# Rounding a kernel's weight parts in the transfer itself, and one product over both parts of the moving operand

## The chip, the core and the metric

The kernel runs on one core of a Trainium2 chip. The metric is the device time of one launch, in microseconds (us), as the median of several runs. One further execution was recorded by the hardware profiler; every duration below is from that execution. PE is the matrix engine (PEld its weight loads), DVE the vector engine, ACT the scalar engine, POOL is GpSimd, and SP issues transfers.

## What is computed

Two layers of a hybrid backbone run over 256 context tokens followed by 256 latent tokens, with width 2048, batch 1 and float32 data. Cut to what matters here:

```
def hybrid_layer(ctx_h, x, ...):
    u_l = rmsnorm(x, norm_w) * (1.0 + scale_l) + shift_l
    u_c = rmsnorm(ctx_h, norm_w) * (1.0 + scale_c) + shift_c
    lx_c, lg_c, q_c, k_c, v_c, ag_c, xbc_c, z_c, dt_c = split_cols(u_c @ w_in)
    lx_l, lg_l, q_l, k_l, v_l, ag_l, xbc_l, z_l, dt_l = split_cols(u_l @ w_in)
    ...   # a gated linear recurrence, windowed attention, a state-space mixer
    mix_l = concatenate([lru_l * silu(lg_l), att_l * silu(ag_l), ssd_l])
    x_new = x + gate_l * (mix_l @ w_out)
    if update_ctx: ctx_h = ctx_h + gate_c * (mix_c @ w_out)      # in the first layer only
```

Most of the work is `u @ w_in` (2048 by 7168, and 16 further columns for dt) and `mix @ w_out` (3072 by 2048) in each layer. The second layer returns no context tokens, so there lg, q, ag, z, the C part of xbc, and all of `w_out` are wanted for the 256 latent tokens alone.

## The kernel before

**Products in three pieces.** Tokens lie along the free dimension: 512 columns in the first layer, 512 or 256 in the second. A weight block is 128 by 128. PE's fast form of float32 rounds its operands, so both operands are cut in two: `hi`, the rounded value, and `lo`, the rest. `mm3` (L247) then makes three products into one accumulator: hi by u's high part, hi by u's low part, and lo by u's high part. Each product loads its own weights. A tile of 512 columns takes three products of 512, and one of 256 columns three of 256.

**The weight stream.** `blocks` (L233) brings weights in halves of four blocks (128 partitions by 512 numbers, 256 KB). For each half SP issues a transfer into `raw` (five buffers), ACT copies raw to `hi`, which rounds it (four buffers), and DVE subtracts `lo` = raw - hi (four buffers). A raw buffer is free once its subtraction is done; hi and lo buffers are free once PE has read them. Each layer has 224 halves of `w_in` and 96 of `w_out`, 640 in all.

**What sets the order.** PE's instructions stand in the order in which the program is written; the mixers are generators that the main loop resumes at due times (`WAIT`, `pump`) counted on a clock of PE work. On the other engines a scheduler that simulates the program at build time orders the instructions. Each engine works its queue strictly in that order: an instruction that waits holds all behind it.

**Stages of a layer.** The head takes the first column tiles of `w_in` (B, C, x) while the modulation is still being loaded; the body takes the rest (lx with lg, z, k and v, q with ag); then `w_out` runs in three parts of 16 column tiles with 8 blocks each. At the end of a `w_out` tile DVE adds the accumulator, times the gate, to the stream `X` (L1082). The mixers put work on all engines: POOL multiplies in the recurrence (L732, L744, L754), in the rotation of q (L776) and scales the attention weights `prob` (L873). Consumers of a column tile (`ssd_z`, `lru_g`, `att_q`, `att_g`) read the accumulator directly.

Of the kernel before, what the change touches and what calls it, by code (L numbers as in the profile page):

```python
# [9 lines left out]
F32R = mybir.dt.float32r  # L10
# [103 lines left out]
for _tag, _bufs, _roles in [  # L114
        ("raw", 5, ("raw",)),
# [16 lines left out]
HB = 4  # L132
# [8 lines left out]
class Kernel:  # L141
# [91 lines left out]
    def blocks(self, src, n_tiles):  # L233
        nc = self.nc
        for i in range(n_tiles):
            whole = src[i].rearrange("p (b c) -> p b c", b=8)
            for h in range(2):
                part = self.t([P, 4, P], "raw")
                nc.sync.dma_start(out=part, in_=whole[:, 4 * h:4 * h + 4])
                hi = self.t([P, 4, P], "hi", HB, F32R)  # L240
                lo = self.t([P, 4, P], "lo", HB, F32R)
                nc.scalar.activation(out=hi, in_=part, func=AF.Copy)  # L242
                nc.vector.tensor_tensor(out=lo, in0=part, in1=hi.bitcast(F32), op=ALU.subtract)  # L243
                for b in range(4):
                    yield hi[:, b], lo[:, b]

# [187 lines left out]
    def u_tile(self, shape=(P, 512)):  # L434
        return self.t(list(shape), "u", 32, F32R)

    def split(self, src, w):
        nc = self.nc
        hi, lo = self.u_tile(), self.u_tile()
        nc.scalar.activation(out=hi[:, :w], in_=src, func=AF.Copy)  # L440
        nc.vector.tensor_tensor(out=lo[:, :w], in0=src, in1=hi[:, :w].bitcast(F32), op=ALU.subtract)
        return hi, lo


    def make_u(self, k, xs, rb, mod):
# [6 lines left out]
        hi, lo = self.u_tile(), self.u_tile()  # L452
# [7 lines left out]
        return hi, lo  # L460


    def conv(self, dst, px, w, b, segs):
# [74 lines left out]
    def ssd_dt(self, l, us, wds):  # L538
        nc = self.nc
        acc = self.ada_acc()  # L540
        for k in range(KT):
            lhsT = wds[k // 8][:, 32 * (k % 8):32 * (k % 8) + P]
            self.mm(acc, lhsT, us[k][0], k == 0, False)
            self.mm(acc, lhsT, us[k][1], False, k == KT - 1)
            self.pump()
# [104 lines left out]
    def ssd_z(self, l, i, pz, t0):  # L650
        nc = self.nc
        th = self.t([P, 512], "cth")[:, t0:]
# [94 lines left out]
    def lru_g(self, l, m, pg, t0):  # L747
        nc = self.nc
        th = self.t([P, 512], "lgt", 1)[:, t0:]
# [61 lines left out]
    def att_q(self, l, h, pq, t0):  # L811
# [4 lines left out]
        sq = self.t([P, 512], "sq", 2)  # L816
        nc.scalar.activation(out=sq[:, t0:], in_=pq, func=AF.Square)
# [83 lines left out]
    def att_g(self, l, h, pg, t0):  # L901
        nc = self.nc
        th = self.t([P, 512], "agt", 1)[:, t0:]
# [10 lines left out]
    def mix_tiles(self, l, part):  # L914
# [17 lines left out]
        for k in range(8):  # L932
            load(k + 4)
            hi, lo = self.split(self.Y[:, k, w0:] if part == 2 else staged[k], n)
            yield hi[:, :n], lo[:, :n]
# [19 lines left out]
    def layer(self, l, xs):  # L955
# [7 lines left out]
        wst = self.blocks(self.a["w_in"][l], NW)  # L963
# [35 lines left out]
        for ct, ks in head_plan(l):  # L999
            fill = ct in FILL[l]  # L1000
            acc = self.mx() if fill else accs[ct][:, cols(ct)]
            for k in ks:
# [22 lines left out]
                self.mm3(acc, next(wst), us[k][0][:, cols(ct)], us[k][1][:, cols(ct)], k == (ks[0] if fill else 0),  # L1025
# [19 lines left out]
        for ct in body(l):  # L1045
# [5 lines left out]
            acc = self.acc()[:, s:]  # L1051
            for k in range(KT):
                self.mm3(acc, next(wst), us[k][0][:, s:], us[k][1][:, s:], k == 0, k == KT - 1)
# [12 lines left out]
        for pi, part in enumerate(OUT_PARTS):  # L1066
# [3 lines left out]
            for m in range(KT):  # L1070
                acc = self.acc()[:, w0:]
                for k in range(8):
                    mix = self.ahead(l, part, min(8, k + 2))[k]
                    self.mm3(acc, next(wo), mix[0], mix[1], k == 0, k == 7)
# [4 lines left out]
                for c, s in ((1, slice(0, C)), (0, slice(C, T))):  # L1079
                    if s.start < w0:  # L1080
# [201 lines left out]
```

## Time and profile before

| | |
|---|---|
| median of 3 runs | 1828.84 us (1825.97 to 1830.53) |
| profiled execution, its own time | 1825.69 us |
| span in that execution | 1823.7 us |
| mean granted share of PE's clock | 0.993 |
| HBM read, written | 310.38 MB, 10.63 MB |
| GpSimd transfers | none |

The span is what the trace covers; the profiled execution lasted 2.0 us more than its span. In the views, a line such as L175 is where the instruction was written; L175 is the helper that every product goes through, so products are told apart by the tiles they write and read: `acc<-u,hi` is a product of the weight stream's high part, `mx<-...` mostly the mixers' work. A matrix instruction's end is modelled, and consecutive ones overlap, so the rate of a stream is read from a run's length divided by its count, not from an instruction's duration. The time of the first 100 us or so is that of the loads; from there on PE has work all the time.

### The profile page before, as it was taken

The numbers are of one execution on the slowest core, as the hardware profiler recorded it, in microseconds if no ns is written. First come the engines' busy times: TensorE is split into PE (matmuls) and PEld (weight loads), VectorE is DVE, ScalarE is ACT, GpSimd is POOL, SyncE is SP. The second block draws the span as 40 slices with busy tenths as digits, with TensorE's granted clock in tenths as the row PEclk, the third lists the DMA queues.
The fourth block names the chain that finished last, engine by engine and source line by source line (L and its number), as shares of the span: only waits on it lengthen the run. The fifth ranks groups of instructions, "written<-read, shape, count | busy, mean of one in ns | idle before, by whom it ended". The sixth has DMA issues, their size and how long they took to land.

```text
span 1823.7 us, 30174 instructions
## 1 busy us (share of the span) xinstructions
PE 1762.9 (97%) x10522; PEld 1449.8 (79%) x10522; DVE 1406.0 (77%) x3117; ACT 972.9 (53%) x1798; POOL 215.5 (12%) x179
## 2 busy tenths in 40 slices
PE   7999999999999999999999999999989999999999
PEld 4677876667778778887888887888767788999999
DVE  4447769898898888889999536877788785788665
ACT  4324578688523354555232335544788863678443
POOL 0000111111110021212000020001122120121000
PEclk9999999999999999999999999999999999999999
DMA  9982333334675645557777433464343564554655
GB/s 359 389 299 66 123 104 104 122 122 144 230 222 179 189 153 184 173 174 239 229 225 225 144 122 107 140 197 148 99 134 113 173 220 137 182 180 153 218 185 179
DMA packets 186343, 322.99 MB, mean 177 GB/s; under 512 B 19120, under 2 KB 44624, under 8 KB 185552
## 3 DMA queue, kind: packets, MB, share of 16 engines
q1 hardware_dynamic: 186192, 321.09, 54.0%
q8 instruction: 82, 1.34, 0.3%
q14 instruction: 69, 0.57, 0.1%
HBM read 310.38 MB, written 10.63 MB: 176 GB/s over the span
## 4 chain that ended last, share of the span: by engine, by line
PE 71%; DVE 9%; issue 8%; ACT 6%; DMA 5%; POOL 1%; SPq 0%; ACTq 0%; DVEq 0%; POOLq 0%
PE acc L175 56%; PE mx L175 12%; PE ada L175 2%; DVE lo L243 2%; DMA bc<-acsD 2%; PE mx L171 1%; DVE araw L385 1%; ACT hi L242 1%; DVE ada L385 1%; DVE lh L735 1%; DMA araw<-in_adaw_dram 1%; DMA ar<-in_ada_dram 1%; DVE ee L1170 1%; ACT ww L1172 1%; ACT lt L717 1%
## 5 line engine op out<-in xcount | busy, mean ns | idle before, releaser
L175 PE MATMUL acc<-u,hi 128*128 128x512 f32 (+1 forms) x4800 | 1278.0, 355 | 3.8 <-ACT u L457 3.0
L175 PEld LDWEIGHTS acc<-u,hi 128*128 128x128 f32 x4800 | 837.5, 190 | 149.4 <-issue 33.2
L175 PE MATMUL acc<-u,lo 128*128 128x512 f32 (+1 forms) x2400 | 843.0, 351 | 7.9 <-DVE lo L243 7.8
L242 ACT ACTIVATE hi<-raw 128x512 fp32r<-128x512 f32 x640 | 397.5, 628 | 536.4 <-PE acc L175 401.3
L243 DVE TENSOR_TENSOR lo<-raw,hi 128x512 fp32r<-128x512 f32 x640 | 456.8, 717 | 185.9 <-ACT hi L242 175.3
L175 PEld LDWEIGHTS acc<-u,lo 128*128 128x128 f32 x2400 | 455.4, 190 | 73.1 <-DVE lo L243 12.9
L385 DVE SCALAR_TENSOR_TENSOR araw<-araw,adac 128x512 f32<-128x512 f32 x256 | 184.3, 720 | 6.2 <-DMA araw<-in_adaw_dram 3.9
L385 DVE SCALAR_TENSOR_TENSOR ada<-araw,adac 128x512 f32<-128x512 f32 x192 | 140.1, 730 | 13.2 <-DMA araw<-in_adaw_dram 6.7
L175 PE MATMUL mx<-u,hi 128*128 128x512 f32 (+1 forms) x320 | 98.8, 392 | 0.0
L1082 DVE SCALAR_TENSOR_TENSOR X<-acc,mod,X 128x256 f32<-128x256 f32 x144 | 65.0, 478 | 40.2 <-PE acc L175 40.2
L732 POOL TENSOR_TENSOR lt<-lt,ltl 128x512 f32<-128x512 f32 x32 | 45.9, 1457 | 327.2 <-ACT ltl L729 304.9
L873 POOL TENSOR_SCALAR prob<-prob,qrs 128x512 f32<-128x512 f32 (+1 forms) x48 | 58.2, 1228 | 214.0 <-ACT hi L242 123.9
L432 POOL TENSOR_TENSOR ssq<-ssq,sq 128x512 f32<-128x512 f32 (+1 forms) x26 | 34.0, 1310 | 308.1 <-ACT sq L428 308.1
L175 PEld LDWEIGHTS mx<-u,hi 128*128 128x128 f32 x320 | 55.9, 188 | 14.0 <-issue 4.6
L175 PE MATMUL mx<-u,lo 128*128 128x512 f32 (+1 forms) x160 | 60.7, 379 | 0.0
L516 POOL TENSOR_SCALAR X<-xs,prm 128x512 f32<-128x512 f32 (+1 forms) x16 | 16.3, 1024 | 362.0 <-DVE xs L494 357.5
L175 PE MATMUL mx<-xc,gw 64*64 64x512 f32 x128 | 41.7, 622 | 8.8 <-ACT lt L717 5.3
L428 ACT ACTIVATE sq<-X 128x256 f32<-128x256 f32 (+1 forms) x44 | 18.8, 452 | 54.5 <-DVE X L659 52.8
L1170 DVE SCALAR_TENSOR_TENSOR ee<-bc,nacs,ee 128x128 f32<-128x128 f32 x96 | 34.8, 418 | 14.8 <-DMA bc<-acsD 9.1
L776 POOL TENSOR_TENSOR qw<-qw,cst 128x256 f32<-128x256 f32 x20 | 23.1, 1156 | 195.6 <-DVE rt L775 168.9
L717 ACT ACTIVATE lt<-mx,gbh 128x512 f32<-128x512 f32 x64 | 42.2, 674 | 4.1 <-PE mx L175 4.0
L1169 ACT ACTIVATE ee<-bc,nacs 128x128 f32<-128x128 f32 x96 | 30.6, 391 | 17.7 <-DMA bc<-acsD 17.7
(240 smaller groups left out, 1946.1 us busy)
## 6 DMA issues: line engine op xcount, KB each, us to landing
raw<-in_w_in_dram SPq DMA_DIRECT2D x448, 256.0 KB, 2.8
araw<-in_adaw_dram SPq DMA_DIRECT2D x256, 256.0 KB, 3.1
raw<-in_w_out_dram SPq DMA_DIRECT2D x192, 256.0 KB, 3.0
ar<-in_ada_dram SPq DMA_DIRECT2D x84, 256.0 KB, 5.4
bc<-acsD SPq DMA_DIRECT2D x48, 256.0 KB, 3.9
ar<-in_ada_dram SPq DMA_DIRECT2D x22, 512.0 KB, 7.0
adac<-condD SPq DMA_DIRECT2D x28, 256.0 KB, 4.4
gw<-in_gates_dram SPq DMA_DIRECT2D x16, 256.0 KB, 2.9
```

The lines of the kernel that those rows point to most:

```text
L175: self.nc.tensor.matmul(out=out, lhsT=lhsT, rhs=rhs, start=start, stop=stop, **kw)
L242: nc.scalar.activation(out=hi, in_=part, func=AF.Copy)
L243: nc.vector.tensor_tensor(out=lo, in0=part, in1=hi.bitcast(F32), op=ALU.subtract)
L385: i = nc.vector.scalar_tensor_tensor(out=o, in0=raw, scalar=1.0, in1=row[c].rearrange("p t x -> p (t x)"), op0=ALU.mult, op1=ALU.mult, acc ...
L432: nc.gpsimd.tensor_tensor(out=self.ssq[0], in0=self.ssq[0], in1=sq, op=ALU.add)
L717: nc.scalar.activation(out=t, in_=pg[g], func=AF.Tanh, scale=0.5, bias=self.gb[:, 16 * g + 8 * d + m:16 * g + 8 * d + m + 1])
L732: nc.gpsimd.tensor_tensor(out=ti, in0=ti, in1=tl[:, d], op=ALU.mult)
L776: nc.gpsimd.tensor_tensor(out=dst, in0=src, in1=self.con("cos"), op=ALU.mult)
L873: nc.gpsimd.tensor_scalar(out=pr[j], in0=pr[j], scalar1=rs[:, j:j + 1], scalar2=1.0, op0=ALU.mult, op1=ALU.mult)
L1082: nc.vector.scalar_tensor_tensor(out=x[:, s], in0=acc[:, s.start - w0:s.stop - w0], scalar=mod[:, 2 * KT + m, c:c + 1], in1=x[:, s], op0=A ...
L1169: nc.scalar.activation(out=e[:, j], in_=bcs[0][:, j], func=AF.Identity, bias=k.nacs[:, f:f + 1])
L1170: nc.vector.scalar_tensor_tensor(out=e[:, j], in0=bcs[1][:, j], scalar=k.nacs[:, r:r + 1], in1=e[:, j], op0=ALU.add, op1=ALU.min)
```

## The change

There are two edits.

**Rounding by the transfer.** `blocks` gets a parameter `own`. For the first `own` pairs of halves ACT rounds as before; for all others GpSimd issues a second transfer of the same half, from the float32 weights in HBM straight into the float32r tile `hi`, which converts on the way. `own` is 20 for the first layer's `w_in` (40 halves, the 160 blocks of its head) and 0 elsewhere: 600 halves of 640 are fetched twice. DVE still subtracts `lo` from raw and hi. The buffers change: raw has three in place of five, hi six in place of four, lo four as before.

**One product over both parts of u.** The two parts of u now lie in one tile [128, 2, 512]. For the second layer's 256-column tiles in the body (lg, z, q, ag: 32 tiles of 16 blocks) and for all of its `w_out` (48 tiles of 8 blocks), `mm_wide` makes one product of hi with both parts, 512 columns into two halves of the accumulator, and one of lo with u's high part into the first half. The two halves are added later: by a new DVE reduction (`whole`) ahead of the consumer in the body, and by a second DVE update of X per `w_out` tile. The C tiles in the second layer's head still go through `mm3`.

```diff
-        ("raw", 5, ("raw",)),
+        ("raw", 3, ("raw",)),
...
-    def blocks(self, src, n_tiles):
+    def blocks(self, src, n_tiles, own=0):
...
                 nc.sync.dma_start(out=part, in_=whole[:, 4 * h:4 * h + 4])
-                hi = self.t([P, 4, P], "hi", HB, F32R)
-                lo = self.t([P, 4, P], "lo", HB, F32R)
-                nc.scalar.activation(out=hi, in_=part, func=AF.Copy)
+                hi = self.t([P, 4, P], "hi", 6, F32R)
+                lo = self.t([P, 4, P], "lo", 4, F32R)
+                if i < own:
+                    nc.scalar.activation(out=hi, in_=part, func=AF.Copy)
+                else:
+                    nc.gpsimd.dma_start(out=hi, in_=whole[:, 4 * h:4 * h + 4])
                 nc.vector.tensor_tensor(out=lo, in0=part, in1=hi.bitcast(F32), op=ALU.subtract)
...
+    def mm_wide(self, acc, block, u, cols, start, stop):
+        hi, lo = block
+        n = cols.stop - cols.start
+        both = lambda: self.mm(acc.rearrange("p (i t) -> p i t", i=2), hi, u[:, :, cols], start, stop)
+        if not stop:
+            both()
+        self.mm(acc[:, 0:n], lo, u[:, 0, cols], False, False)
+        if stop:
+            both()
...
+    def whole(self, acc, t0, dst):
+        if t0 == 0:
+            return acc
+        self.nc.vector.tensor_reduce(out=dst[:, 0:t0], in_=acc.rearrange("p (i t) -> p t i", i=2), axis=AX.X, op=ALU.add)
+        return dst[:, 0:t0]
...
+        pz, th = self.whole(pz, t0, th), th[:, t0:]
...
+        wst = self.blocks(self.a["w_in"][l], NW, 0 if l else 20)
...
+                if s:
+                    self.mm_wide(acc, next(wst), us[k], slice(s, T), k == 0, k == KT - 1)
+                else:
+                    self.mm3(acc, next(wst), us[k][:, 0], us[k][:, 1], k == 0, k == KT - 1)
...
+                late = slice(C, T)
+                for c, s, o in ((0, late, 0), (0, late, n)) if l else ((1, slice(0, C), 0), (0, late, C)):
+                    nc.vector.scalar_tensor_tensor(out=x[:, s], in0=acc[:, o:o + C], scalar=mod[:, 2 * KT + m, c:c + 1],
+                                                   in1=x[:, s], op0=ALU.mult, op1=ALU.add)
```

PE, in the last `w_out` tile of the second layer, before: two blocks, three products each (u's two parts are tiles of their own).

```order
L175 MATMUL acc_19442<-u_18704,hi_19445 128x256
L175 MATMUL acc_19442<-u_18705,hi_19445 128x256
L175 MATMUL acc_19442<-u_18704,lo_19446 128x256
L175 MATMUL acc_19442<-u_18710,hi_19445 128x256
L175 MATMUL acc_19442<-u_18711,hi_19445 128x256
L175 MATMUL acc_19442<-u_18710,lo_19446 128x256
```

PE at the same place after: three blocks of the same tile.

```order
L174 MATMUL acc_18553<-u_17948,hi_18556 128x512
L174 MATMUL acc_18553<-u_17948,lo_18557 128x256
L174 MATMUL acc_18553<-u_17953,hi_18556 128x512
L174 MATMUL acc_18553<-u_17953,lo_18557 128x256
L174 MATMUL acc_18553<-u_17987,hi_18556 128x512
L174 MATMUL acc_18553<-u_17987,lo_18557 128x256
```

A block has two products where it had three, over the same 768 columns.

DVE, in the second layer's `w_out`, before. The tiles' accumulators follow each other as 18623, 18667, 18715, 18763; a lo belongs to the tile whose accumulator's number is next below its own, so lo_18737 is the second half of tile 18715.

```order
L1082 SCALAR_TENSOR_TENSOR X_17512<-acc_18623,mod_33_146,X_17512 128x256
L243 TENSOR_TENSOR lo_18737<-raw_18734,hi_18736 128x512
L243 TENSOR_TENSOR lo_18767<-raw_18764,hi_18766 128x512
L1082 SCALAR_TENSOR_TENSOR X_17512<-acc_18667,mod_33_146,X_17512 128x256
L243 TENSOR_TENSOR lo_18785<-raw_18782,hi_18784 128x512
L243 TENSOR_TENSOR lo_18815<-raw_18812,hi_18814 128x512
```

DVE in the same stage after; the accumulators follow each other as 17851, 17882, 17919, 17958.

```order
L1113 SCALAR_TENSOR_TENSOR X_16968<-acc_17851,mod_33_146,X_16968 128x256
L246 TENSOR_TENSOR lo_17923<-raw_17920,hi_17922 128x512
L1113 SCALAR_TENSOR_TENSOR X_16968<-acc_17882,mod_33_146,X_16968 128x256 x2
L246 TENSOR_TENSOR lo_17937<-raw_17934,hi_17936 128x512
L246 TENSOR_TENSOR lo_17962<-raw_17959,hi_17961 128x512
L1113 SCALAR_TENSOR_TENSOR X_16968<-acc_17919,mod_33_146,X_16968 128x256 x2
```

Before, the update of tile m is followed by the second half of tile m+2; after, both updates of tile m (17882) are followed by the second half of tile m+1 (17919). The two updates stand next to each other in 31 of the 48 tiles, and around a lo in the others.

POOL, among the second layer's q tiles, before: the rotation of one head and the scaling of another's weights, in turn.

```order
L776 TENSOR_TENSOR qw_16139<-qw_16139,cst_76 128x256
L873 TENSOR_SCALAR prob_16263<-prob_16263,qrs_16262 128x512
L873 TENSOR_SCALAR prob_16265<-prob_16265,qrs_16262 128x512
L776 TENSOR_TENSOR qw_16376<-qw_16376,cst_76 128x256
L873 TENSOR_SCALAR prob_16492<-prob_16492,qrs_16491 128x512
```

POOL at such a place after; each transfer waits until PE has read the half six before it.

```order
L245 DMA hi_16464<-in_w_in_dram 128x512
L245 DMA hi_16524<-in_w_in_dram 128x512
L899 TENSOR_SCALAR prob_16286<-prob_16286,qrs_16285 128x512
L899 TENSOR_SCALAR prob_16288<-prob_16288,qrs_16285 128x512
L245 DMA hi_16555<-in_w_in_dram 128x512
L245 DMA hi_16569<-in_w_in_dram 128x512
L801 TENSOR_TENSOR qw_16388<-qw_16388,cst_76 128x256
```

The mixers' POOL work now stands between transfers for which the weight stream waits; POOL has 600 such transfers beside 174 instructions of the mixers.

## Rows read from the trace of the kernel before

**Rows 1.** Page: busy us of the engines; then GB/s in 40 slices.
```profile
PE 1762.9 (97%) x10522; PEld 1449.8 (79%) x10522; DVE 1406.0 (77%) x3117; ACT 972.9 (53%) x1798; POOL 215.5 (12%) x179
...
GB/s 359 389 299 66 123 104 104 122 122 144 230 222 179 189 153 184 173 174 239 229 225 225 144 122 107 140 197 148 99 134 113 173 220 137 182 180 153 218 185 179
```

**Rows 2.** Chain that ended last: start us, length us, engine, line, count; two runs.
```profile
...
898.55 213.56 PE acc L175 x942
...
1698.32 122.06 PE acc L175 x1017
```

**Rows 3.** Groups by form, whole span: count | busy us, mean ns.
```profile
...
L175 PE MATMUL acc<-u,hi 128*128 128x512 f32 x2976 | 943.4, 398 | 3.8 <-ACT u L457 3.0 <-DVE u L458 0.8
...
L175 PE MATMUL acc<-u,hi 128*128 128x256 f32 x1824 | 335.0, 285 | 0.0
```

**Rows 4.** Waits of PE, 100 to 1824 us: total us, times, longest us.
```profile
...
PE mx L175 <- ACT lt L717: 11.9, 8, 4.2
PE acc L175 <- DVE lo L243: 7.8, 10, 1.6
PE mx L175 <- DVE ee L1176: 4.2, 2, 3.1
...
PE mx L171 <- POOL prob L873: 3.4, 4, 2.2
...
PE mx L175 <- ACT sq L817: 0.3, 1, 0.3
```

**Rows 5.** The same view of 1440 to 1490 us alone.
```profile
...
PE acc L175 <- DVE lo L243: 4.4, 4, 1.6
```

**Rows 6.** Waits of ACT, then of DVE, 100 to 1824 us, same columns.
```profile
...
ACT hi L242 <- PE acc L175: 394.0, 277, 6.3
...
DVE lo L243 <- ACT hi L242: 149.2, 138, 3.6
```

**Rows 7.** Busy us by stretch: PE, PEld, DVE, ACT, POOL; clock, DMA share, GB/s.
```profile
...
1220.00:1440.00 220.00, 206.91 (x1189) 160.33 (x1187) 172.44 (x315) 156.38 (x281) 32.35 (x28) 0.98 0.40 129
1440.00:1490.00 50.00, 45.46 (x346) 39.43 (x345) 41.24 (x66) 40.34 (x66) 14.10 (x12) 1.00 0.62 201
1490.00:1690.00 200.00, 199.04 (x1449) 187.95 (x1449) 152.60 (x350) 128.88 (x251) 33.65 (x29) 1.00 0.54 174
1698.00:1821.00 123.00, 122.36 (x1020) 122.15 (x1018) 79.47 (x133) 53.87 (x90) 0.00 (x0) 1.00 0.60 188
```

**Rows 8.** Groups by form of 1698 to 1821 us, DVE and ACT.
```profile
...
L243 DVE TENSOR_TENSOR lo<-raw,hi 128x512 fp32r<-128x512 f32 x81 | 56.1, 692 | 29.7 <-ACT hi L242 27.4
L242 ACT ACTIVATE hi<-raw 128x512 fp32r<-128x512 f32 x81 | 51.1, 631 | 61.6 <-PE acc L175 61.6
L1082 DVE SCALAR_TENSOR_TENSOR X<-acc,mod,X 128x256 f32<-128x256 f32 x43 | 20.8, 483 | 11.9 <-PE acc L175 11.9
```

**Rows 9.** DVE in order of time: start us, length us, [idle before, releaser].
```profile
...
1751.28 0.48 DVE L1082 SCALAR_TENSOR_TENSOR X<-acc,mod,X 128x256 f32<-128x256 f32 x1 [0.20 <-PE acc L175]
1751.82 0.69 DVE L243 TENSOR_TENSOR lo<-raw,hi 128x512 fp32r<-128x512 f32 x1
```

**Rows 10.** Transfers: mean rate, us from issue to landing; 1698:1821, then 20:85.
```profile
...
DMA packets 13975, 23.12 MB, mean 188 GB/s; under 512 B 1539, under 2 KB 3971, under 8 KB 13964
...
raw<-in_w_out_dram SPq DMA_DIRECT2D x77, 256.0 KB, 3.1
...
DMA packets 11970, 24.87 MB, mean 383 GB/s; under 512 B 1339, under 2 KB 1627, under 8 KB 11961
...
raw<-in_w_in_dram SPq DMA_DIRECT2D x19, 256.0 KB, 5.7
```

**Rows 11.** POOL's dearest, a DVE reduction, SP's issues of raw (min/median/max ns).
```profile
L732 POOL TENSOR_TENSOR lt<-lt,ltl 128x512 f32<-128x512 f32 x32 | 45.9, 1457 | 327.2 <-ACT ltl L729 304.9 <-DVE araw L385 22.3
...
L851 DVE TENSOR_REDUCE qmx<-mx 128x1 f32<-128x512 f32 x32 | 20.9, 680 | 0.1
...
L239 SPq DMA_DIRECT2D raw<-in_w_out_dram x77: 327/328/489, 1697.9 to 1808.7; - x77
```

More of the change, by code (lines that the diff above doesn't have):

```diff
@@ L459, in make_u @@
                                            op0=ALU.add, op1=ALU.subtract)
[L460 removed]
+        return u
     def conv(self, dst, px, w, b, segs):
@@ L748, in lru_g @@
         nc = self.nc
-        th = self.t([P, 512], "lgt", 1)[:, t0:]
+        th = self.t([P, 512], "lgt", 1)
+        pg, th = self.whole(pg, t0, th), th[:, t0:]
         nc.scalar.activation(out=th, in_=pg, func=AF.Tanh, scale=0.5)
@@ L816, in att_q @@
         sq = self.t([P, 512], "sq", 2)
+        pq = self.whole(pq, t0, qw)
         nc.scalar.activation(out=sq[:, t0:], in_=pq, func=AF.Square)
@@ L902, in att_g @@
         nc = self.nc
-        th = self.t([P, 512], "agt", 1)[:, t0:]
+        th = self.t([P, 512], "agt", 1)
+        pg, th = self.whole(pg, t0, th), th[:, t0:]
         nc.scalar.activation(out=th, in_=pg, func=AF.Tanh, scale=0.5)
@@ L933, in mix_tiles @@
             load(k + 4)
-            hi, lo = self.split(self.Y[:, k, w0:] if part == 2 else staged[k], n)
-            yield hi[:, :n], lo[:, :n]
+            yield self.split(self.Y[:, k, w0:] if part == 2 else staged[k], n)
     def ahead(self, l, part, n):
@@ L1024, in layer @@
                         self.prms.append(self.params(1))
-                self.mm3(acc, next(wst), us[k][0][:, cols(ct)], us[k][1][:, cols(ct)], k == (ks[0] if fill else 0),
+                self.mm3(acc, next(wst), us[k][:, 0, cols(ct)], us[k][:, 1, cols(ct)], k == (ks[0] if fill else 0),
                          k == (ks[-1] if fill else KT - 1))
@@ L1050, in layer @@
                 self.att_begin(l)
-            acc = self.acc()[:, s:]
+            acc = self.acc()
             for k in range(KT):
-                self.mm3(acc, next(wst), us[k][0][:, s:], us[k][1][:, s:], k == 0, k == KT - 1)
+                if s:
+                    self.mm_wide(acc, next(wst), us[k], slice(s, T), k == 0, k == KT - 1)
+                else:
+                    self.mm3(acc, next(wst), us[k][:, 0], us[k][:, 1], k == 0, k == KT - 1)
                 if ct == ("ag", 7) and OUT_PARTS[0] in self.parts_done:
@@ L1070, in layer @@
             for m in range(KT):
-                acc = self.acc()[:, w0:]
+                acc = self.acc()
                 for k in range(8):
                     mix = self.ahead(l, part, min(8, k + 2))[k]
-                    self.mm3(acc, next(wo), mix[0], mix[1], k == 0, k == 7)
+                    if l:
+                        self.mm_wide(acc, next(wo), mix, slice(0, n), k == 0, k == 7)
+                    else:
+                        self.mm3(acc, next(wo), mix[:, 0], mix[:, 1], k == 0, k == 7)
                     self.pump()
@@ L1078, in layer @@
                 x = xs[m // 8][:, m % 8]
-                for c, s in ((1, slice(0, C)), (0, slice(C, T))):
-                    if s.start < w0:
-                        continue
-                    nc.vector.scalar_tensor_tensor(out=x[:, s], in0=acc[:, s.start - w0:s.stop - w0],
-                                                   scalar=mod[:, 2 * KT + m, c:c + 1], in1=x[:, s], op0=ALU.mult,
-                                                   op1=ALU.add)
+                late = slice(C, T)
+                for c, s, o in ((0, late, 0), (0, late, n)) if l else ((1, slice(0, C), 0), (0, late, C)):
+                    nc.vector.scalar_tensor_tensor(out=x[:, s], in0=acc[:, o:o + C], scalar=mod[:, 2 * KT + m, c:c + 1],
+                                                   in1=x[:, s], op0=ALU.mult, op1=ALU.add)
                 if pi == 2:
```

19 lines of the change are left out of this document (9 added, 10 removed).

## The prediction

> **What bounds the kernel now.** I read the busy shares first, then the chain, then who waits for whom, then single stages. PE is busy 97% of the span, DVE 77%, ACT 53%, POOL 12% [rows 1]. A busy PE can still be a slow one, so its two long undisturbed runs in the chain are the measure: 942 products of 512 columns in 213.56 us, or 0.227 us each, and 1017 of 256 columns in 122.06 us, or 0.120 us each [rows 2]. After the first 100 us PE waits little: the 15 lines of its waits, of which the first and the last stand there, sum to 43.1 us [rows 4], of which 15.2 end on ACT (11.9 of them on the gates' `lt`), 7.8 on DVE's `lo` (4.4 in the z tiles of the second layer alone [rows 5]), 16.7 on other work of DVE and 3.4 on POOL's `prob`. So the program is PE's stream plus some 43 us, and an edit gains by shortening that stream or by those waits, and by nothing else.
>
> What rounding on ACT costs is mostly not its 631 ns [rows 8]: an ACT rounding stands in a strict queue until PE gives back a hi buffer, 394.0 us in 277 waits, and DVE's `lo` then waits for ACT another 149.2 us [rows 6]. All work of the mixers behind them on ACT and DVE waits along.
>
> **One product over both parts.** A 256-column block takes 3 x 0.120 = 0.360 us now and 0.227 + 0.120 = 0.347 after, so 0.0133 us less; for 32 x 16 + 48 x 8 = 896 blocks that is 11.9 us. A product costs 13 ns beyond its columns at 2.4 GHz in both runs (0.2267 against 0.2133, 0.1200 against 0.1067), and one product in three goes. The Trainium skill's TensorE: Matmul & The Clock Gate (Back-to-back issue gap) has N/2.4 + 2.5 ns instead; by that one product less would save only 2.5 ns a block, an estimate of 2.2 us in all and a total 9.7 us later. This trace doesn't agree with the page (13 ns), and I take the trace.
>
> The 11.9 us fall in three places: 5.1 in lg, q and ag (384 blocks), 1.7 in z (128), 5.1 in `w_out` (384). In lg, q and ag they are PE's to keep, since lx or attention stand between them and leave the supply time. In the other two a half of weights is used up in 4 x 0.347 = 1.39 us, and supply has to be looked at.
>
> **Supply in z and `w_out` of the second layer.** Three limits, each per half:
> The raw buffers. A raw buffer is taken from issue to landing, 3.1 us, and through the subtraction, 0.69 us and some 0.05 between [rows 8, 10]: 3.84 us, by five buffers 0.77 us, by three 1.28 us. That is still under 1.39, but the transfers now move twice the weights: 188 GB/s there now and some 189 more (262 KB in 1.39 us), against 383 GB/s in the start, where landing took 5.7 us [rows 10]. With 5.7 us the three buffers give one half per 2.15 us. I take 3.7 us, nearer the low end, since in the start some fifteen buffers of other loads were in flight and here it is three raws and a hi or two: 1.48 us per half.
> DVE's order. It does both updates of X before the next `lo`. From the start of a tile's last product: its duration 0.398 [rows 3], two updates of 0.48 with 0.06 behind each, and 0.69 for `lo` [rows 9], 2.17 us. PE can fill 0.227 + 1.387 + 0.227 = 1.84 us of it, until the second half's `lo` is wanted. So 0.33 us are short in each of the 31 tiles where both updates come first, 10 us. Before, that `lo` was made a whole tile earlier.
> POOL's issue. The trace of before has no GpSimd transfer. The low end for one is SP's issue, 0.33 us, the high end POOL's dearest instruction, 1.457 us [rows 11]. I take 1.0; only the high end is over 1.39.
> Together: `w_out` takes PE 96 x 1.387 = 133 us, with DVE's 10 or the buffers' 96 x 1.48 = 142 some 146, as the two shortfalls mostly fall together, where it takes 96 x 1.44 = 138 now: **+8 us** (from -5 with no shortfall to +68 at 2.15 us). z takes 32 x 1.48 = 47 where it is 46 + 4.4 of waits now: **-3 us** (-6 to +18).
>
> **What ACT gives back.** 600 roundings of 0.63 us leave ACT, 379 us, with the 394 us of waits on PE, and DVE no longer waits for ACT. Of PE's 43.1 us, 35.3 lie outside z and POOL. From 1220 to 1440 us ACT is busy 156 of 220 us and DVE 172 [rows 7]; ACT falls by a third, DVE doesn't, and `lo` still stands in DVE's queue, now for a transfer. The bounds are 0 and 35; I take 11 of the 15.2 us that end on ACT and 3 of the rest: **-14 us**. The 40 halves that ACT keeps cover the first layer's head, so the start, where the engines of the transfers are full, stays as it is: 0.
>
> **What goes to POOL.** 600 issues at 0.33 to 1.457 us are 200 to 870 us beside its 215 us: not a bound of the whole. But `prob`, the rotation and the recurrence now stand behind transfers that wait for PE. PE waits 3.4 us for `prob` now; with one issue of 1 us, part of the time, in each of 16 heads I add **+5 us** (0 to +16).
>
> **The new reductions.** 32 of about 0.68 us [rows 11] in place of nothing, 22 us on DVE; in 1490 to 1690 us DVE is busy 153 of 200 us [rows 7], and 16 of them fall there. Hidden by 47 us of idle time; if DVE were full they would cost at most the 11 us there: 0.
>
> **The sum**: -5 (lg, q, ag) - 3 (z) + 8 (`w_out`) - 14 (ACT) + 5 (POOL) = -9 us. Against the profiled execution that is 1825.7 - 9 = 1817; that execution lay 3 us under the median of its runs, so on the median 1828.8 - 9 = **1820 us**.
>
> **The rivals.**
> A, slower: the converting transfer takes the transfer engines longer than a copy. 262 KB at 383 GB/s is 0.68 us of all engines; if converting doubles it, a half costs 0.68 + 1.37 = 2.05 us, and the 128 halves of z and `w_out` in the second layer take 128 x (2.05 - 1.44) = 78 us more. With the other terms (-5 - 14 + 5, and 4 in z) 1889 us. It decides from 1.58 us per half, where 128 x 0.14 us eat those 18. For it: no row shows such a transfer, and at equal cost the engines would already be at 377 of 383 GB/s. Against: the sizes stay the same, 2 KB a row.
> B, slower by less: three raw buffers under that load. A landing of 4.4 us gives 1.71 us per half, 128 x 0.27 = 35 us more, and 1845 us. For it: the two landings in rows 10; against: nothing else is loaded in these stages.
> C, no change: the waits on ACT turn into waits on DVE, which stays as full as it was, and only 5 us of product gain meet 8 of `w_out`: 1823 to 1834.
> D, a larger gain: PE's loads are the bound. The weight loads are busy 122.15 of 123 us in `w_out` [rows 7]. The Trainium skill's Trainium Kernel Development and Optimization (Performance Expectations) says that the busy share of weight loads is a good measure of how close a kernel is to its limit, and that of matmuls a bad one. If loads held PE back, dropping one in three would leave the columns alone, 768 at 2.4 GHz or 0.320 us a block: 896 x 0.040 = 36 us in place of 11.9, and with the waits about 1790. Against it: products of 512 columns, whose loads have twice the time, lose the same 13 ns. A gain of that size would come as well if most of the 35 us of waits went.
>
> **Chances.** What the measurement can tell from no change is about 0.3%, 5.5 us. The forecast, 1806 to 1823: 0.35. D, under 1806: 0.12. C: 0.19. B, 1834 to 1870: 0.17. A, over 1870: 0.17. So faster 0.47, the same 0.19, slower 0.34. The range of 1798 to 1880 leaves out some 0.06 below and 0.13 above; the likeliest case alone has 1806 to 1823.
>
> **What would show it.** In the profile after: runs of 512 and 256 in turn at 0.347 us a block in lg, q and ag; `w_out` of the second layer as a stretch of about 146 us, with waits on `lo` and, on DVE, on raw's or hi's landing; ACT busy near 590 us; PE's waits on `lt` under 5 us; POOL at 1 us a transfer. If a hi transfer moves under 2 KB per 0.17 us of an engine, A is out. I am wrong if `w_out` stays at 133 us (then about 1807), if hi lands later than PE takes six halves, 8.3 us, or if PE waits for `prob` far more than 8 us.

## The result, and the profile after

The changed kernel takes 1934.1 us, the median of 4 runs (1931.2 to 1938.5), against 1829.7 before (one more run than the three of the table above): a ratio of 1.058, 95% interval 1.055 to 1.060, 5.8% slower. The forecast was 1820 with a range of 1798 to 1880; the sign and the size were both wrong. The profiled execution has a span of 1935.9 us, 112.2 more than the one of before; it was the longest of its four runs, and the one of before lay under all of its own, so 112 us in the profiles stand for 104 in the medians.

The page of the changed kernel, with the rows that answer to [rows 1]: busy time of the engines, the rate in 40 slices, the two queues, and two of the transfers' groups (KB each, median us from issue to landing).

```profile
PE 1799.7 (93%) x9626; PEld 1413.9 (73%) x9626; DVE 1440.3 (74%) x3197; ACT 634.7 (33%) x1198; POOL 520.9 (27%) x779
...
GB/s 360 363 265 105 218 179 170 201 179 282 275 253 218 245 229 258 243 259 323 309 307 273 219 194 235 282 251 193 178 196 267 290 237 267 239 247 282 287 296 250
...
q1 hardware_dynamic: 186192, 321.09, 50.4%
q0 software_dynamic: 86400, 157.32, 29.0%
...
raw<-in_w_out_dram SPq DMA_DIRECT2D x192, 256.0 KB, 4.4
hi<-in_w_out_dram POOLq DMA_DIRECT2D x192, 256.0 KB, 4.8
```

ACT lost the work that it was meant to lose, 973 to 635 us, and POOL is far from full. PE waits more. The waits of PE, 100 to 1936 us (us in total, times, longest), which answer to [rows 4]:

```profile
PE acc L174 <- DVE lo L246: 52.2, 63, 2.4
PE mx L174 <- ACT lt L741: 16.5, 7, 3.8
PE mx L174 <- ACT qh L855: 11.8, 7, 2.7
PE mx L174 <- DVE rs L428: 7.3, 3, 6.1
PE mx L174 <- ACT sq L843: 6.8, 5, 2.9
PE mx L170 <- POOL prob L899: 5.8, 7, 2.5
```

In 7.8 us of [rows 4] PE waited for `lo`; now in 52.2. The gates' `lt`, for which ACT was to be freed, went from 11.9 to 16.5 us, the attention's `qh` is new, and its `sq` went from 0.3 to 6.8.

Where the 112 us lie, worked out from the start times of PE's first product on `lo` of each stage's first half (in us; the last column is a later run, no_raw, which has the converting transfers without the second stream of bytes):

| stage (halves) | before | after | difference | no_raw |
|---|---|---|---|---|
| layer 1, first 40 | 162.2 | 162.8 | +0.6 | 163.1 |
| layer 1, to the end of lx, lg (72) | 280.4 | 274.3 | -6.1 | 268.4 |
| layer 1, z (32) | 93.4 | 104.0 | +10.6 | 100.3 |
| layer 1, k, v (16) | 53.8 | 63.3 | +9.6 | 56.0 |
| layer 1, q, ag (64) | 231.9 | 234.9 | +3.0 | 232.7 |
| layer 1, w_out (96) | 271.2 | 277.3 | +6.2 | 271.2 |
| layer 2, head (48) | 138.4 | 135.1 | -3.3 | 138.7 |
| layer 2, lx, lg (64) | 193.5 | 199.1 | +5.5 | 187.2 |
| layer 2, z (32) | 55.1 | 70.2 | +15.0 | 53.8 |
| layer 2, k, v (16) | 48.8 | 49.0 | +0.2 | 48.8 |
| layer 2, q, ag (64) | 122.8 | 152.8 | +30.0 | 132.8 |
| layer 2, w_out to the end (96) | 146.0 | 186.9 | +40.9 | 146.8 |

So 86 us lie in the three stages of the second layer that use a half up fastest, and 20 in the first layer's z, k and v. `w_out` of the second layer in the changed kernel, first by stretch as in [rows 7] (the other lines are 1477 to 1547, z, and 1596 to 1749, q and ag), then the waits in it:

```profile
1477.00:1547.00 70.00, 53.90 (x274) 38.93 (x272) 50.47 (x81) 19.13 (x31) 31.89 (x48) 1.00 0.91 280
1596.00:1749.00 153.00, 132.65 (x727) 111.80 (x726) 108.78 (x258) 60.84 (x125) 52.57 (x86) 0.94 0.83 251
1749.00:1936.00 187.00, 155.57 (x800) 121.40 (x798) 115.46 (x223) 9.16 (x22) 49.38 (x93) 0.98 0.92 278
```
```profile
POOL hi L245 <- PE acc L174: 97.2, 67, 6.5
DVE lo L246 <- DMA raw<-in_w_out_dram: 50.6, 47, 2.8
PEld acc L174 <- DVE lo L246: 43.5, 58, 2.2
PE acc L174 <- DVE lo L246: 23.3, 32, 1.8
```

No engine is busy 90% of that stretch but the transfer engines, 92% at 278 GB/s. DVE waits 50.6 us for the landing of raw, and PE behind it for lo; in [rows 8] 27.4 of its 29.7 us ahead of `lo` were for ACT. hi is mostly there in time (from 1740 to 1930 us DVE waits 1.7 us for its landing): POOL issues it early and waits for PE to give buffers back. One such wait in order of time (start us, length us, what, [idle before, releaser]):

```profile
1794.18 3.27 SPq L239 DMA_DIRECT2D raw<-in_w_out_dram  x2
...
1796.40 0.69 DVE L246 TENSOR_TENSOR lo<-raw,hi 128x512 fp32r<-128x512 f32 x1 [1.85 <-DMA raw<-in_w_out_dram]
1797.01 1.00 DVE L1113 SCALAR_TENSOR_TENSOR X<-acc,mod,X 128x256 f32<-128x256 f32 x2
1797.15 0.38 PE L174 MATMUL acc<-u,lo 128*128 128x256 f32 x1 [1.27 <-DVE lo L246]
```

### The profile page after: what moved, and what is told of

The parts are those of the page before. It is cut to its first block, busy times and chain, and to the rows that moved or that the text cites. A ratio compares the mean times of both kernels' runs of the same rounds, so it can differ in the third digit from the quotient of the medians.

```text
span 1935.9 us, 28530 instructions
## 1 busy us (share of the span) xinstructions
PE 1799.7 (93%) x9626; PEld 1413.9 (73%) x9626; DVE 1440.3 (74%) x3197; ACT 634.7 (33%) x1198; POOL 520.9 (27%) x779
## 4 chain that ended last, share of the span: by engine, by line
PE 39%; DMA 22%; DVE 22%; issue 10%; ACT 5%; POOL 2%; SPq 0%; DVEq 0%; POOLq 0%; ACTq 0%
PE acc L174 27%; PE mx L174 9%; DMA raw<-in_w_out_dram 6%; DVE lo L246 6%; DMA araw<-in_adaw_dram 5%; DVE araw L399 3%; DVE ada L399 3%; DMA hi<-in_w_in_dram 3%; DMA raw<-in_w_in_dram 3%; PE ada L174 2%; DMA bc<-acsD 2%; DMA adac<-condD 1%; DVE X L1113 1%; POOL hi L245 1%; ACT prob L889 1%
## 5 line engine op out<-in xcount | busy, mean ns | idle before, releaser
L174 PE MATMUL acc<-u,hi 128*128 128x512 f32 x3904 | 1281.4, 401 | 5.0 <-ACT u L473 3.3
L174 PE MATMUL acc<-u,lo 128*128 128x512 f32 (+1 forms) x2400 | 844.1, 357 | 53.3 <-DVE lo L246 52.2
L174 PEld LDWEIGHTS acc<-u,hi 128*128 128x128 f32 x3904 | 729.0, 191 | 179.8 <-issue 33.6
L245 POOL DMA_DIRECT2D hi<-in_w_in_dram x408 | 221.0, 542 | 839.3 <-PE acc L174 572.0
L245 POOL DMA_DIRECT2D hi<-in_w_out_dram x192 | 102.1, 532 | 320.7 <-PE acc L174 283.1
L1113 DVE SCALAR_TENSOR_TENSOR X<-acc,mod,X 128x256 f32<-128x256 f32 x192 | 88.1, 479 | 39.8 <-PE acc L174 38.5
L174 PEld LDWEIGHTS mx<-u,hi 128*128 128x128 f32 x320 | 56.3, 190 | 14.1 <-issue 5.0
L899 POOL TENSOR_SCALAR prob<-prob,qrs 128x512 f32<-128x512 f32 (+1 forms) x48 | 48.9, 1031 | 14.8 <-DVE qrs L893 9.5
L723 ACT ACTIVATE xsw<-xc 64x512 f32<-64x512 f32 x32 | 20.2, 630 | 66.0 <-DVE xc L487 47.6
```

The costliest lines, as they stand in the source:

```text
L174: self.nc.tensor.matmul(out=out, lhsT=lhsT, rhs=rhs, start=start, stop=stop, **kw)
L245: nc.gpsimd.dma_start(out=hi, in_=whole[:, 4 * h:4 * h + 4])
L723: nc.scalar.activation(out=xs[r:r + 64], in_=xc[o:o + 64], func=AF.Copy)
L899: nc.gpsimd.tensor_scalar(out=pr[j], in0=pr[j], scalar1=rs[:, j:j + 1], scalar2=1.0, op0=ALU.mult, op1=ALU.mult)
L1113: nc.vector.scalar_tensor_tensor(out=x[:, s], in0=acc[:, o:o + C], scalar=mod[:, 2 * KT + m, c:c + 1], in1=x[:, s], op0=ALU.mult, op1=ALU.add)
```

## The experiments

Theory S: the supply of weights is what was lost, since the transfers move them twice. Its rivals were DVE's order and the new sums, the converting itself, and GpSimd's strict queue. Ratios are to the kernel before, on the same chip.

**The two edits apart.** cast_only keeps the transfers and drops `mm_wide` and the sums; wide_only keeps these and rounds everything on ACT.

```
cast_only   mm_wide: three products into acc[:, 0:n]; whole: return acc[:, 0:t0]; one update of X
wide_only   blocks: nc.scalar.activation(hi, part) for every half; raw 5, hi 4
```

> The changed kernel with its converting transfers and its buffers (3 raw, 6 hi, 4 lo), but with three products of 256 columns a block and one update of X a tile, as in the kernel before. Theory S (the supply of weights is what was lost: a half now comes every 1.95 us in w_out of the second layer, whatever PE does with it): the 96 halves of that w_out stay at about 187 us, the 64 of q and ag at about 150, and the whole lies at 1925 to 1945, as the changed kernel's 1934. Rival O (what was lost is DVE's order, two updates of X and the new reductions ahead of lo): w_out falls to 150 or less, q and ag to 130, and the whole to 1870 to 1890.

> The other half alone: one product over both parts of u, the reductions and the two updates of X, with every half rounded on ACT from raw, 5 raw and 4 hi buffers as before. Theory S: supply is the old one, so the products' 12 to 13 us stay, less what two updates of X ahead of lo cost; 1815 to 1822 in all, w_out of the second layer about 140 us and below 146, q and ag about 120. Rival O: w_out at 160 or more and the whole above 1840.

cast_only: 1917.5 us, ratio 1.046 (1.042 to 1.050), with `w_out` at 184.9 us as theory S has it: the supply loses the time there, whatever PE does. The whole lies 7 us under S's range, since q and ag fell to 138.2: of their 30 us only 15 are left without the wide product and its sums, which S had not said (no_raw divides these 15 once more). wide_only: 1840.1 us, 1.0036 (1.0023 to 1.0049). Its `w_out` is 143.5 us, within S's bounds, but the whole is 18 us above S's range, just at rival O's edge, without the `w_out` of 160 that O wanted: q and ag took 131.9 in place of 122.8, which no theory had. The edits alone lose 86 and 8 us; both at once lose 104.

**What carries the supply: buffers, converting or the bytes.**

```
bufs553     raw 3 -> 5, hi 6 -> 5, lo 4 -> 3
no_convert  gpsimd.dma_start(out=hi, in_=weights.bitcast(F32R))
half_cast   bufs553, and: if i < own or i % 2: ACT rounds
raw_pool    kernel before, raw by gpsimd.dma_start (plain copy), ACT rounds
no_raw      cast_only, no raw transfer behind tile 20; lo = hi - hi
```

> The changed kernel with 5 raw, 5 hi and 3 lo buffers in the place of 3, 6 and 4 (13 buffers of 2 KB in each). Theory S1 (three raw buffers: issue and landing 4.4, wait behind DVE's other work 0.7, lo 0.7, so 5.85 us a buffer and 1.95 a half): five give 1.17 us, PE's 1.39 decides, w_out of the second layer 135 to 150 us, the whole 1830 to 1860. Theory S2 (the 16 transfer engines are full: a half is 128 packets of about 100 ns and 128 of about 115, 1.72 us of all engines, with 94% of them busy in that stage): w_out stays at 165 to 187, landing grows beyond 6 us, the whole 1900 to 1935.

bufs553: 1913.0 us, 1.0445 (1.042 to 1.047); `w_out` 174.4 us, S2 by its bounds. Its `w_out` by stretch and in waits:

```profile
1736.00:1910.00 174.00, 154.17 (x798) 122.71 (x796) 115.61 (x223) 8.75 (x21) 50.55 (x94) 0.98 0.96 299
```
```profile
DVE lo L246 <- DMA hi<-in_w_out_dram: 23.8, 34, 3.1
```

With five raw buffers DVE's longest wait for a landing is hi's, not raw's any more, and the transfer engines are busy 96%. The new buffers take 12.5 of the 41 us off `w_out` and 21 off the whole; as hi and lo have one less each, what three raw buffers cost by themselves isn't shown. At 5.0 us of landing, with the 0.7 and 0.7 of the expectation, a ring of five would give a half per 1.28 us; one came per 1.81. Landing times grew to 5.0 us for raw and 5.2 for hi, not beyond 6 as expected.

> The changed kernel with the same GpSimd transfers of 256 KB into hi, but without conversion: they copy the weights' bits unrounded (so hi is the whole weight and lo is zero; the products use them so). Tells the price of converting from that of moving the weights twice. If converting is what costs (2 KB packets of GpSimd's queue 99 ns and more, 84 for a copy): those packets fall to about 84 to 100 ns mean, w_out of the second layer to 165 to 175 us, the whole to 1895 to 1915. If the second transfer as such costs (landings, three raw buffers): w_out at 180 to 190 and the whole within 0.5% of the changed kernel's 1934.

no_convert: 1941.0 us, 1.060 (1.057 to 1.063), and `w_out` 187.3 us. The run can't decide what it was made for: naming the source fp32r didn't make the transfer a plain one. The Trainium skill's DMA: Bandwidth & Descriptors (SWDGE vs HWDGE vs iDMA) says that a float32r source is read as float32, so that such a destination always converts. The trace agrees: hi's queue took 44.9% of 16 engines for 23.86 MB in 187 us, 56.3 us of an engine a MB, and 56.6 in the changed kernel (45.1%). So it is only a second run of the change, and no run here moves the weights twice without converting.

> The kernel before, with the raw transfers issued by GpSimd in the place of SyncE: the same bytes, no conversion, ACT rounds. It separates the price of GpSimd's queue from that of converting. Theory Qu (the queue costs): its 2 KB packets take 98 to 99 ns in the middle as the converting ones do, and an issue 0.53 us of GpSimd. Theory Cv (converting costs): they take 84 ns as SyncE's. For the time, if GpSimd's strict order is what holds the mixers up (a transfer waits for its buffer and rotation, prob and the recurrence stand behind it): POOL's prob and its like cost PE 5 to 15 us more, 1835 to 1850; if not, 1827 to 1835.

raw_pool: 1839.5 us, 1.0042 (1.0026 to 1.0058), in the range for a strict order on GpSimd that costs something, though PE's waits for `prob` only went from 3.4 to 4.5 us. By its packet records it is theory Cv, though they carry 4 KB, which neither theory had: 159 ns in the middle, 80 ns for 2 KB, where a converting packet of 2 KB takes 99. The queue rows of `w_out`, 146 to 147 us each: of the kernel before (a plain copy by SyncE, with the other transfers of the stage), raw_pool (a plain copy by GpSimd), no_raw (converting), with packets, MB, share of 16 engines:

```profile
q1 hardware_dynamic: 17371, 27.55, 59.7%
```
```profile
q0 software_dynamic: 7084, 23.18, 52.6%
```
```profile
q0 software_dynamic: 13104, 23.86, 62.5%
```

That is 0.526 x 16 x 147 / 23.18 = 53.4 us of an engine a MB for a copy and 61.6 for a converting transfer, in stages of nearly equal bytes: 15% more, not twice, the smaller packets included. GpSimd's queue as such is hardly dearer: SyncE's took 0.597 x 16 x 146 / 27.55 = 50.6 in the kernel before.

> As bufs553 (the changed kernel with 5 raw, 5 hi and 3 lo buffers), but of the tiles of weights behind the first 20 every second one is rounded on ACT from raw, so only half of the converting transfers are left. Theory E (the transfer engines are full where PE uses weights up fastest): a half then takes them 128 x 100 ns / 16 = 0.80 us for raw, half of 0.93 for hi and some 0.15 for the rest, 1.41 us, just PE's 1.39; w_out of the second layer falls from 174 to 138 to 150 us, its landings from 4.6 towards 3.5 us, z to below 60, the whole to 1840 to 1865. Rival H (the path of a converting transfer is what is slow, not the engines' load: its queue, its hi buffer that comes late, GpSimd's order): every second tile still waits for it, and w_out stays above 160 us, the whole above 1880.

half_cast: 1876.4 us, 1.026 (1.023 to 1.028); `w_out` 160.5 us, z 59.6, q and ag 145.1. z came in E's range and `w_out` just in H's; the whole met neither and lies between, and raw's landing of 4.2 us, too. The engines were no longer full there (the kernel before, then half_cast):

```profile
1678.00:1824.00 146.00, 141.80 (x1181) 141.40 (x1179) 96.82 (x175) 68.22 (x121) 2.06 (x2) 1.00 0.60 190
```
```profile
1712.00:1872.00 160.00, 146.63 (x800) 122.67 (x798) 111.97 (x221) 36.26 (x66) 26.24 (x48) 0.98 0.81 248
```

In all-engine time a half (share x stretch / 96) this is 0.81 x 160 / 96 = 1.35 us, between 0.91 before (0.60 x 146) and 1.79 after (0.92 x 187): half the converting transfers cost half. What keeps `w_out` 14 us long at 81% isn't shown by a run of its own. DVE still waits 14.9 us there for hi's landing and 13.7 for PE, and ACT's roundings wait 77.6 us for raw's.

> As cast_only (converting transfers behind the first 20 tiles, three products a block, 3 raw, 6 hi, 4 lo), without the raw transfers of those tiles: lo is made on DVE at the same place and of the same size, as hi minus hi (so the lo part of the weights is left out of the result). GpSimd's queue, its 600 converting transfers, the hi buffers, DVE's and PE's work all stay; half of the bytes go. Theory E (raw and hi together fill the transfer engines, and raw's three buffers then come too late): w_out of the second layer falls from 185 to 140 to 150 us with the engines about 50% busy, q and ag from 138 to 120 to 126, z from 68 to 55 to 58, landings of hi to 3 to 3.5 us, the whole to 1805 to 1835, where the lower end would be ACT's relief of some 14 us or more with nothing against it. Rival H (the converting path itself, its queue on GpSimd or its landing, holds PE up): w_out stays above 165 us and the whole above 1880.

no_raw decides between E and H: 1831.7 us, 0.9992 (0.998 to 1.0004), `w_out` 146.8, z 53.8. All of the converting path is in it, the 600 issues, their queue, hi's landing, DVE's lo, and nearly the whole 86 us of cast_only are gone with the second stream of bytes. The ring of three raw buffers went with that stream; that the bytes weigh more than the ring is read from bufs553, which with five raw buffers is still 81 us slower than the kernel before, at 96% busy engines. The `w_out` of no_raw:

```profile
1679.00:1826.00 147.00, 142.94 (x1186) 142.32 (x1184) 92.03 (x165) 8.73 (x21) 49.41 (x93) 1.00 0.71 190
```

Some figures of theory E were off: z came a little under its range, the engines are 71% busy, not 50%, and q and ag stayed at 132.8 us. Their stretch in cast_only, then in no_raw, and PE's waits in no_raw's:

```profile
1591.00:1729.00 138.00, 127.98 (x979) 121.40 (x979) 100.75 (x236) 56.19 (x113) 54.24 (x86) 0.98 0.90 273
```
```profile
1547.00:1679.00 132.00, 125.30 (x977) 119.54 (x976) 108.05 (x250) 59.84 (x125) 51.60 (x86) 0.99 0.60 165
```
```profile
PE mx L174 <- ACT qh L852: 3.8, 4, 2.7
PE mx L174 <- DVE ql L853: 2.8, 6, 0.6
```

So of cast_only's 15.4 us in q and ag only 5.4 go with the bytes; 10.0 stay at engines that are 60% busy. The run also gives what ACT's relief brings where the second stream is gone, less what GpSimd's queue costs (raw_pool, with that queue alone, lost 7 us): nothing. lx and lg are 12.0 and 6.4 us shorter, and the first layer's z (+7.0) and the second's q and ag (+10.0) give it back.

**Is there a stage where the transfers gain?** Layer 1's lx and lg were shorter in every kernel with them and six or five hi buffers (268 to 277 us against 280).

```
cast_early  kernel before (raw 5, hi 4, lo 4); converting transfers in tiles 20 to 55 of layer 1 alone
early_463   the same with raw 4, hi 6, lo 3
```

> The kernel before (three products a block, 5 raw, 4 hi, 4 lo) with converting transfers in one stage alone: tiles 20 to 55 of the first layer's w_in, where cast_only was 9 us shorter than the kernel before (271 against 280). Theory G (there ACT is the crowded engine and the transfer engines have room, so the gain belongs to the stage): that stage stays at 270 to 275 us and all others as before, 1820 to 1826 in all. Rival B (the gain needs six hi buffers, since a hi buffer is taken from the issue on): with four, GpSimd waits for PE and lo for hi; the stage stays at 278 or more and the whole at 1828 or more.

> As cast_early (three products a block, converting transfers only in tiles 20 to 55 of the first layer's w_in), with 4 raw, 6 hi and 3 lo buffers in the place of 5, 4 and 4. Theory Hb (a converting transfer takes its hi buffer from the issue on, so it needs more of them than ACT's rounding: with 4 that stage took 291 us, with 5 276, with 6 271, against 280 rounded by ACT): the stage falls to 268 to 274 us, the others stay as before, and the whole lies at 1820 to 1827, some 5 to 9 us under the kernel before. Rival R (what made cast_only short there was something else that hangs on the later stages, or four raw buffers are too few for ACT's roundings): stage above 277, or w_out of the second layer above 152, and 1830 or more.

cast_early: 1846.0 us, 1.0076 (1.0061 to 1.0091), the stage at 291.3 us, 11 longer: rival B. early_463: 1852.3 us, 1.0106 (1.0086 to 1.0126). The stage falls to 272.5, as Hb has it: a converting transfer takes its hi buffer from the issue on, so it wants more of them. But the later stages, where ACT rounds with one raw and one lo buffer less, lose it again (z of layer 1 +7.0, z of layer 2 +5.5, q and ag +8.1). That the gain in the stage is ACT's relief isn't shown: raw_pool, where ACT rounds everything, takes 274.8 us there.

**What the wide product pays.**

```
wide_no_q   wide_only, q by three products and without its reduction
wide_bare   wide_only without reductions and without the second update of X
wide_out    wide_only, mm_wide in w_out alone
```

> As wide_only (ACT rounds every half, one product over both parts of u), but the q tiles of the second layer are made by three products of 256 columns and without a reduction. Theory Q (wide_only's 9 us more in q and ag come from the reduction that each q now needs ahead of its square and its copy: attention starts later and PE waits for sq, qh and ql): those waits, 8 us in wide_only, fall under 2 us, q and ag go from 131.9 to 121 to 124 us, and the whole from 1840 to 1827 to 1832. Rival L (16 reductions are too much load on DVE there): half of it stays, q and ag at 126 to 129, the whole at 1833 to 1837.

> As wide_only (ACT rounds all halves, one product over both parts of u), with the sums of the two halves left out: no reduction, and one update of X a tile, which takes the first half alone (u's second part is left out of the result). What is left is the products' own gain. Theory P (13 ns a block, as the strides of the traces show, 0.345 against 0.360 us a block): 896 blocks give 12 to 13 us, q and ag fall from 131.9 to 116 to 119 us, w_out of the second layer to 139 to 142, and the whole to 1816 to 1821; the sums are then what wide_only paid 19 us for. Rival N (the products' gain is taken back by PE's waits elsewhere, whatever DVE does): 1827 or more.

> ACT rounds all halves (5 raw, 4 hi, 4 lo); one product over both parts of u in w_out of the second layer alone, with its two updates of X a tile; lg, z, q and ag by three products and without reductions. In wide_only and wide_bare PE's clean time in that w_out was 134 us against 138 before. Theory P: that stage is 2 to 4 us shorter than the 146 of before, all others as before, 1826 to 1831, the fastest of all, though hardly clear of the kernel before. Rival N: the end of attention, which runs under w_out, or two updates of X ahead of lo take it back; 1831 or more.

wide_no_q: q and ag fall from 131.9 to 124.4 us, at theory Q's upper end, with 2.5 us of those waits left, but the whole only to 1837.7, 1.0025 (1.0013 to 1.0037), outside both ranges; in its trace the end of attention fell into `w_out`, which took 150.1. wide_bare: 1829.7 us, 0.9987 (0.9977 to 0.9997), q and ag 119.6, without a wait of PE there. So the sums, the reductions and the second update together, cost 1840.1 - 1829.7 = 10 us, and q and ag alone are 131.9 - 119.6 = 12.3 us longer with them. Of the products' 12 us only 3 are seen: rival N by the whole. wide_out: 1830.0 us, 0.9983 (0.9973 to 0.9994), 2 us under the kernel before on its chip (1832.2), the fastest kernel here that computes the whole result, by less than the 0.3% that is to be told from no change. Its profiled `w_out` was 146.7 us, so the stage itself doesn't show those 2 us.

PE's waits in q and ag, 1564 to 1696 us in wide_only, where the kernel before has 0.3 us for `sq` in all:

```profile
PE mx L174 <- ACT qh L855: 4.3, 2, 3.6
PE mx L174 <- ACT sq L843: 2.6, 4, 1.0
PE mx L174 <- DVE ql L856: 1.2, 3, 0.5
```

The longest run of products in wide_only's chain, to be held against [rows 2] (start us, length us):

```profile
1717.16 118.80 PE acc L174 x674
```

337 blocks in 118.80 us are 0.3525 us a block, against 3 x 0.120 = 0.360: a gain of 7.5 ns, not 13. By the start times of that run the 512-column product takes 0.2355 us ahead of a 256-column one and 0.2346 ahead of another of 512 (41 times, where tiles meet), where [rows 2] have 0.227; the 256-column one takes 0.117. So it isn't the turn of the two sizes that makes it dearer. It differs from the products of [rows 2] in that it reads u in two pieces of 256 columns; that this is the cause isn't shown.

## Why the prediction was wrong, step by step

**The capacity of the transfers, the step that failed.** The prediction set 377 GB/s of need (188 and some 189) against 383 in the start, and on that took a landing near its low end. The row that it needed was there: [rows 7] has `w_out` at 0.60 of the transfer engines for 188 GB/s, so they are full at 188 / 0.60 = 313 GB/s; bufs553 measured 299 at 0.96, cast_only 285 at 0.93, the changed kernel 278 at 0.92, which give 311, 306 and 302. The start's 383 GB/s belong to other transfers (some 43 us of an engine a MB, 1.03 x 16 x 65 / 24.87, where `w_out` pays 50.6; a packet of 2 KB takes 88 ns on average in the start and 104 in `w_out`); why a MB costs more here isn't shown. With 0.91 us of all engines a half from before and 0.87 to 0.88 for a converting one (1.79 - 0.91), a half needs 1.79 us, and PE would use one in 1.39: 96 x 1.79 = 172 us with the engines full, against the 146 forecast and 187 measured at 92%.

**The raw buffers.** The ring was the right second look. Landing was taken at 3.7 us and measured at 4.4 to 4.5 in the middle, 4.55 on average; between landing and lo lie a further 0.63 us on average (0.09 in the middle: in some halves DVE is at other work). With 0.03 from lo's end to the next issue and 0.70 for lo that gives 5.9 us a buffer, 1.97 by three, where a half came every 1.95. B's 4.4 us came true, and B was priced too low, at 1.71 us. The reason for the low end was a miscount: in the start 7.7 transfers were in flight on average and never more than 8, not fifteen of other loads. `w_out` had 2.4 in flight before, at 3.1 us, and 5.1 after, halfway to the start, and halfway to its 5.7 us is where landing came out.

**`w_out` +8, z -3.** Measured +40.9 and +15.0. The z term lay inside its bounds (to +18), the `w_out` term too (to +68). These two bounds alone reach 1901 with the other terms as taken (-5, -14, +5), so the stated range to 1880 was narrower than the working.

**q and ag, no supply loss.** "lx or attention stand between them and leave the supply time" failed: +30.0. A half took 123 / 64 = 1.92 us there, and the engines 0.54 x 1.92 = 1.04 us of it before; with 0.88 more they would be full, 1.92. By that the room was just used up, and the runs divide the loss so: 5.4 us go with the second stream of bytes (cast_only less no_raw), 10.0 stay with the converting transfers alone (no_raw), and 14.6 come with the wide product and its sums, which alone lose 9.1 there (wide_only).

**The first layer: not costed at all.** Its z, k and v lost 20 us. In k and v PE had room, but the modulation's loads share the engines: there the landing of `araw` went from 3.1 to 4.1 us and of `adac` from 4.1 to 6.5. Without the second stream (no_raw) k and v keep 2.2 of their 9.6 us, but z keeps 6.9 of its 10.6, so z's loss is not the bytes' in the main, and its cause stays open. One place in k and v, DVE and then five stretches of the changed kernel:

```profile
609.16 0.70 DVE L399 SCALAR_TENSOR_TENSOR ada<-araw,adac 128x512 f32<-128x512 f32 x1 [5.21 <-DMA adac<-condD]
...
612.83 0.17 DVE L428 RECIPROCAL rs<-rs 128x4 f32<-128x4 f32 x1
```
```profile
600.00:604.00 4.00, 4.00 (x20) 3.30 (x19) 3.85 (x8) 0.65 (x2) 1.55 (x3) 1.00 0.87 272
604.00:608.00 4.00, 3.03 (x18) 2.33 (x16) 0.00 (x0) 0.94 (x2) 0.54 (x2) 1.00 0.84 236
608.00:612.00 4.00, 0.00 (x0) 0.00 (x0) 2.84 (x8) 0.00 (x0) 0.00 (x0) 0.80 0.63 189
612.00:616.00 4.00, 2.85 (x11) 2.69 (x12) 3.71 (x12) 0.00 (x0) 0.00 (x0) 0.50 0.80 242
616.00:620.00 4.00, 4.00 (x17) 3.21 (x16) 3.12 (x9) 0.60 (x1) 0.95 (x2) 0.85 0.42 137
```

DVE stands 5.2 us before a modulation step whose transfer is late; the reciprocal `rs` is queued behind it, and PE waits 6.1 us for that. After PE has stood, the granted clock is 0.50 in the next stretch, the lower of its levels, 1.2 GHz, and two products of 512 columns take 1.00 us there (614.85 to 615.85) where two took 0.45 before (603.25 to 603.70): a wait costs more than its length.

**ACT, -14.** ACT was relieved as forecast (635 us where about 590 was said). The gain came in lx and lg of layer 1 (-6.1; -12.0 in no_raw), and 3.3 us in the second layer's head. `lt` went up, from 11.9 to 16.5 us: its chain runs over the convolution on DVE, for which ACT's copy `xsw` waits 12.2 us from 1220 to 1460 us where it waited 6.8 from 1220 to 1440 before. That this is why `lt` comes later is argued. In no_raw, with the bytes gone, the wait for `lt` fell to 5.2, as the term had it; without the bytes' price the term would have been right in lx and lg and lost in q and ag.

**POOL, +5.** PE's waits for `prob` went from 3.4 to 5.8 us, 2.4 of the 5 taken; an issue takes 0.53 us of POOL (1.0 taken). The rotation of q was named but not priced: in no_raw's q and ag PE waits 3.8 us for `qh` and 2.8 for `ql`, work that stands behind POOL's waits for hi buffers (855 us in the changed kernel). That it is this queue that gives back no_raw's 10 us in q and ag is argued, not shown.

**The reductions, 0.** With the second updates they cost 10 us (wide_only against wide_bare), mostly in q and ag, where 16 of the 32 reductions lie. Hiding them by DVE's idle share was the mistake: the sum stands on the way from PE's accumulator to `sq`, `qw` and `qh`, for which PE soon waits.

**DVE's order, 10 us.** Didn't happen: in wide_only, where the two updates stand next to each other in 43 of the 48 tiles and the supply is that of before, PE waits for lo 0.4 us in `w_out`.

**The product, -11.9.** The sign was right; the run above gives 7.5 ns a block for 13.3, 6.7 us over 896 blocks. The step that failed took the wide product's price from 512-column products that read u in one piece. Rival D is out: the weight loads fell from 141 to 121 us in `w_out` (wide_only) and a block is 0.3525 us, not 0.320.

**The rivals.** A's time (1889) and its point of decision (1.58 us a half) were the nearest to the result, but not for its reason: by the test given for it, 2 KB in under 0.17 us of an engine, converting isn't twice as dear (56.6 us a MB are 0.116 us for 2 KB). What A had for it, "the engines would already be at 377 of 383 GB/s", was the case.

## What to carry to other kernels

Whether a second stream of bytes fits is read from the stage that needs it: its rate divided by its share of the transfer engines is its capacity, and that stage's own 313 GB/s, not the 383 of another stage, had to be held against 377. How long a transfer takes to land goes with how many are in flight: 3.1 us at 2.4, 4.5 at 5.1, 5.7 at 7.7 here. Moving a rounding from an engine to the transfers needs room there, and it asks for more buffers of the result, which are taken from the issue on; one stage was 8 us shorter so (early_463), and no whole kernel here kept it. A short instruction on a half idle engine isn't free if it lies between a product and what PE waits for next.

## What was not expected of the hardware

A converting transfer costs 61.6 us of an engine a MB where a plain copy by the same queue costs 53.4: converting on the way adds 15%. Taking the second stream away brings the landing of hi in `w_out` from 5.0 us (cast_only) to 3.3 (no_raw). A product of 512 columns that reads its columns in two pieces took 0.235 us, 8 ns more than one that reads them in one; why isn't shown. And the granted clock fell to 0.50 behind a wait of PE of 6 us, in a kernel whose mean clock is 0.98.
